# A third pair of buffers for rounded weights, conversion two jobs ahead from the last projection on, and the first spread sums landed in two parts

## Chip, cores, metric

The kernel runs on 1 core of one Trainium2 chip. The metric is the device time of one execution in microseconds (us); lower is better. All times below are us unless marked otherwise. Engines: PE does matmuls, ACT, DVE and POOL work on tensors in SBUF and PSUM, SP issues most of the DMAs.

## The reference

Two layers of a hybrid decoder on 16 learned meta tokens and 512 real ones (528 columns here, 1024 features). Cut to what matters for this change:

```python
proj = einsum('bld,dc->blc', rmsnorm(h, attn_norm_g), w_in)
fq, fk, fv, flog, rq, rk, rv, rg = split(proj)            # FoX group, retention group
logf = log_sigmoid(flog + b_fgate)
c = cumsum(logf, axis=1)                                  # the forget sums, one row per head
s = einsum('bhqd,bhkd->bhqk', q, k) * Dh**-0.5 + c[..., :, None] - c[..., None, :]
fox_out = softmax(mask(s)) @ v
ret_out = silu(rg) * groupnorm(retention(rotate(rq), rotate(rk), rv))
h = h + concatenate([fox_out, ret_out]) @ w_out
hn = rmsnorm(h, ffn_norm_g)
h = h + (silu(hn @ w_gate) * (hn @ w_up)) @ w_down
```

FoX has 8 heads of 64, retention 4 of 128; the feed-forward width is 2816. After both layers comes a last rmsnorm, and the meta tokens are dropped.

## The kernel before, in words

**Products in three parts.** Every float32 weight and activation is split into a rounded high part and the rest (`whi`, `wlo`; `xh`, `xl`), and each product is three matmuls, `xh*whi + xl*whi + xh*wlo` (lines 197 to 230, the matmul itself is L217). So each block of weights is first loaded raw, and then converted: `whi` is an ACT cast (L191), and `wlo` is a subtraction raw - `whi` (L194) on DVE in two pieces of 128x512, or on POOL in eight of 128x128 where the job has `pool`.

**Jobs.** Each 1024x128 block of `w_in`, `w_out`, `w_gate` and `w_up` that `dense_steps` handles is a job j with one raw buffer (ring of 3, loaded by SP with L158, 512 KB) and one pair `whi`, `wlo` (rings of 2, from the pool `wp`). While PE works on job j, its steps 1 and 4 convert the two halves of job j+1. So a raw buffer comes free when the job's conversion is done, and a pair when PE has used it. The later blocks of the feed-forward part come from another code path (lines 869 and 870, names `whi`, `wlo`, `fwhi`, `fwlo`).

**What orders the work.** PE's order is written out by hand: lists of steps are merged by position (`spread`, `merge`). The order on ACT, DVE, POOL and SP is made by a scheduler from what is ready when, with a few places of high priority; so another ring size or an earlier call moves instructions there. Each engine works in its own order and stops at the first instruction whose input is missing. For SP that means that a DMA behind a load waits until the load's raw buffer is free.

**The start of a layer.** `x` is normalised: ACT makes `xh` (L319) and squares, DVE makes `xl` (L320) and the running sum of squares `ss` (L340); `split` (L142 on ACT, L143 on DVE) makes `sqh` and `sql` of it, and PE sums over the partitions (L290). The forget weights are split into `pt` (L142), which POOL has cleared before (L364). In layer 1 POOL also clears the attention buffers (L85, L102) when it enters the attention phase. The first jobs of a layer are q, k and v of the first FoX pair; in layer 0 these are jobs 0, 1 and the ones that follow; in layer 1 q and k are converted by ACT and DVE, and v by ACT and POOL.

**The forget sums.** A scan (L399) makes the sums of all 8 heads, ACT writes them to DRAM (`cdr`, L401), and for each head SP spreads one row of them over 128 partitions (`bc`, L497, 264 KB). `scores` (from L492) needs `bc` in L514, which subtracts it from PE's scores (L507) and finds the row's minimum, `nmax`.

Of the kernel before, what the change touches and what calls it, by code (L numbers as in the profile page):

```python
# [11 lines left out]
F32R = mybir.dt.float32r  # L12
# [4 lines left out]
NK = D // 128  # L17
SEQ = 512
META = 16
# [20 lines left out]
def hybrid_kernel(ctx, tc, x_t, w_in, w_fl, w_out, w_gate, w_up, w_down, vecs, b_fg, rope, decay, mask, ident, out_t):  # L40
# [119 lines left out]

    def wring(tag):
        pool = phase["ffn"] if tag[0] == "f" else wp
        return pool.tile([128, NK, 128], F32R, name=tag, tag=tag, bufs=2)

    def convert(j, upto=NK, pinned=False):

        if j >= len(jobs):
            return
        job = jobs[j]
        fetch(j)  # L170
        if "make" in job:
            if "w" not in job:
                n = job["n"]
                hi, lo = (wring(job["ring"] + p) for p in ("whi", "wlo"))
                job["w"] = [(NK, hi, lo)]
                job["make"](hi[:, 0:n], lo[:, 0:n])
            return
        n = job["src"].shape[1]
        if "w" not in job:
            job["w"] = [(NK, *(job["own"]() if job["own"] else  # L180
                               [wp.tile([128, NK, 128], F32R, name=i, tag=i) for i in ("whi", "wlo")]))]
            job["split"] = 0
        sub = nc.gpsimd.tensor_sub if job["pool"] else nc.vector.tensor_sub
        while job["split"] < min(n, upto):
            c0 = job["split"]
            c1 = min(n, c0 + (2 if j < 2 and c0 < 4 else 4))
            size, hi, lo = job["w"][c0 // job["w"][0][0]]
            o = c0 % size
            hi, lo = hi[:, o:o + c1 - c0], lo[:, o:o + c1 - c0]
            with tc.high_priority() if j == 5 else ExitStack():  # L190
                pin(nc.scalar.copy(hi, job["raw"][:, c0:c1]), pinned)  # L191
            step = 1 if job["pool"] else c1 - c0
            for i in range(0, c1 - c0, step):
                pin(sub(lo[:, i:i + step], job["raw"][:, c0 + i:c0 + i + step], hi[:, i:i + step].bitcast(F32)), pinned)  # L194
            job["split"] = c1

    def dense_steps(src, parts, pool=False, banks=False, ahead=(1, 4), own=None, wait=None):

        j = len(jobs)
        jobs.append({"src": src, "pool": pool, "own": own})

        def chunk(k0, k, n, xs, cols, ps, done):
            def go():
                convert(j)
                if k == 0:
                    t = [psum_a() for _ in cols] if banks else psum()
                    ps.append(t)
                    ps.append(t if banks else [t[:, b] for b in range(2)])  # L210
                size = jobs[j]["w"][0][0]
                _, hi, lo = jobs[j]["w"][(k0 + k) // size]
                wk = (k0 + k) % size
                xh, xl = xs(k)
                for i, (w, x) in enumerate(((hi, xh), (hi, xl), (lo, xh))):
                    for b, (c0, c1) in enumerate(cols):
                        nc.tensor.matmul(ps[1][b][:, 0:c1 - c0], w[:, wk, :], x[:, c0:c1],  # L217
                                         start=(k == 0 and i == 0), stop=(k == n - 1 and i == 2))
                if k == n - 1:
                    done(ps[0]) if wait is None else wait.append(lambda: done(ps[0]))  # L220
                for half, at_step in enumerate(ahead):
                    if k0 + k == at_step:
                        convert(j + 1, 4 * half + 4)
            return go

        steps = []
        for k0, xs, n, cols, done in parts:
            ps = []
            steps += [chunk(k0, k, n, xs, cols, ps, done) for k in range(n)]
        return steps  # L230
# [239 lines left out]
    def fox_steps(g, st, ly, real):  # L470
# [21 lines left out]
        def scores(s, b):  # L492
            nq, nk, q0 = span(b)
            if b == blocks[0]:
                bc = at("bc", F32, bufs=2)
                hd = 2 * g + s
                nc.sync.dma_start(bc, ly["cdr"][hd:hd + 1, :].partition_broadcast(128))  # L497
                st["bc"] = bc
            bc = st["bc"]
            segs = FULL if nk == T else ((0, nk),)  # L500
            pt = take(pm_tiles, "pm") if b < 0 else p_tiles[b]
            mins = []
            normalise()
            for c0, c1 in segs:
                sc = psum_a()
                for i, kk in enumerate(st["k"][s]):
                    nc.tensor.matmul(sc[0:nq, 0:c1 - c0], st["q"][s][:, q0:q0 + nq], kk[:, c0:c1],  # L507
                                     start=(i == 0), stop=(i == 1))
                nm = tmp.tile([128, 1], F32, name="nmax", tag="nmax", bufs=6)
                with tc.high_priority():  # L510
                    if c1 == nk:
                        diag = sc[0:nq, c1 - c0 - nq:c1 - c0]
                        nc.vector.tensor_add(diag, diag, msk[0:nq, 0:nq])
                    nc.vector.tensor_tensor_reduce(pt[0:nq, c0:c1], sc[0:nq, 0:c1 - c0], bc[0:nq, c0:c1],  # L514
                                                   -1.0, 3.0e38, ALU.add, ALU.min, nm[0:nq])
                mins.append(nm)
            nmax = mins[0]
            if len(mins) > 1:
                nc.vector.tensor_tensor(nmax, mins[0], mins[1], ALU.min)
            if b < 0:  # L520
                rsum = tmp.tile([META, 1], F32, name="rsum", tag="rsum", bufs=4)
            else:
                if (s, b) == (0, 0):
                    st["sums"] = tmp.tile([128, NBLK, 2], F32, name="sums", tag="sums")
                rsum = st["sums"][:, b, s:s + 1]
            pr = pt[0:nq, 0:nk]
            nc.scalar.activation(pr, pr, AF.Exp, bias=nmax[0:nq], scale=-1.0, accum_out=rsum)  # L527
            info[s, b] = pt
            if b == NBLK - 1:
                st["ct"] = tmp.tile([32, NBLK, 32], F32, name="ct", tag="ct")  # L530
                nc.vector.transpose(st["ct"], p_tiles[NBLK][96:128, :, WP - 32:WP])
            if b < 0:
                info["open"] = (pr, rsum)
            elif (s, b) == todo[-1]:
                nc.vector.reciprocal(st["sums"], st["sums"])
                st["rows"] = tt("tq")
                nc.scalar.copy(st["rows"][:, 0:SEQ].rearrange("p (b s d) -> p b s d", b=NBLK, s=2),
                               st["sums"].unsqueeze(3).broadcast_to([128, NBLK, 2, 64]))
# [248 lines left out]
    def out_proj(l, rnd, mix, real):  # L787

        cols = REAL if real else FULL
        xs = lambda k: mix[k]["mix"]  # L790
        return sum([dense_steps(w_out[l, rnd, m2], [(4 * s, xs, 4, cols, add_h(2 * m2 + s, real)) for s in range(2)],
                                rnd == 0 or m2 < 2, rnd == 1 and m2 == 1) for m2 in range(NK // 2)], [])

    def ffn(l, st, real, last):
        QC = REAL if real else FULL
# [234 lines left out]
        for r, (f0, f1) in enumerate(ROUNDS):  # L1030
            for f in range(f0, f1):
                if f < PLAIN:
                    steps += dense_steps(w_gate[l, f], [(0, xs, NK, QC, g_done(f) if f else held.append)], banks=f == 1)
                    steps += dense_steps(w_up[l, f], [(0, xs, NK, QC, u_done(f))])
                    continue
                u = Unit(f)
                steps += u.head()
                for v in tails:
                    v.last()
                    steps += v.tail()  # L1040
                tails = []
                u.rest()
                steps += u.middle()
                if fills:
                    p, g0, g1 = fills.pop(0)
                    j = down_job(p, g0, g1)
                    steps += down(j, 0, 2 * p, g0, g1, not real)
                    u.last()
                    steps += u.tail()
                    steps += down(j, 1, 2 * p + 1, g0, g1, False)  # L1050
                else:
                    tails = [u]
            for p, g0, g1 in fills:
                j = down_job(p, g0, g1)
                for s in range(2):
                    steps += down(j, s, 2 * p + s, g0, g1, False)
            fills = [(p, f0, f1) for p in range(NK // 2)]
# [348 lines left out]
```

## Time and profile before

| What | Value |
|---|---|
| median of 3 runs | 1271.39 (1270.4 to 1271.77) |
| the profiled execution, its own time | 1271.32 |
| its span in the trace | 1269.5 |
| mean granted clock of PE | 0.999 |
| weight loads of `w_in`, issue to landing, median | 3.5 (54 loads of 512 KB) |
| spreading `bc`, issue to landing, median | 3.5 (16 of 264 KB) |

The span runs from the first to the last instruction of the trace; 1.8 of the execution's own time lie around it. "Busy" counts the time in which an engine has an instruction in work. In a timeline, a row gives the start, the time to the end of the group, the engine, the line, the operation with output and inputs, the count, and in brackets how long the engine had been idle ahead of it and what ended that. SPq is SP's queue: its long rows of several DMAs hold the waits between them.

### The profile page before, as it was taken

What the parts mean: (1) busy time and instruction counts of PE and PEld (TensorE: products, weight loads), DVE (VectorE), ACT (ScalarE), POOL (GpSimd) and SP (SyncE); (2) the same over time, 40 slices, a digit from 0 to 9 for tenths busy, and PEclk for the clock granted to TensorE, in tenths of its full rate; (3) what the DMA queues carried; (4) which work ended last, traced back from release to release, by engine and by line L of the source; (5) the groups of instructions that cost most, each with busy time, mean ns of one, the idle gap of its engine ahead of it and who ended that gap; (6) DMA issues with size and microseconds to landing.
All of it is one profiled execution on the core that took longest, in us unless ns stands there. A gap on an engine that the chain in (4) does not pass through costs nothing.

```text
span 1269.5 us, 23615 instructions
## 1 busy us (share of the span) xinstructions
PE 1255.6 (99%) x9271; PEld 1197.8 (94%) x9271; DVE 997.3 (79%) x1843; ACT 687.7 (54%) x1246; POOL 264.0 (21%) x522
## 2 busy tenths in 40 slices
PE   9999999999999999999999999999999999999997
PEld 8999999999999999999999989998789999999996
DVE  7877756779988888887786877567899888888866
ACT  6666545676444444444456665557764444444444
POOL 3355546420000000000025545454100000000000
PEclk9999999999999999999999999999999999999999
DMA  6222232223333333332323232222323333333321
GB/s 217 93 69 86 88 87 73 70 68 114 107 97 100 100 100 101 100 100 84 101 76 119 62 99 83 80 88 68 101 95 120 100 100 100 101 100 100 104 80 67
DMA packets 45680, 120.57 MB, mean 95 GB/s; under 512 B 5360, under 2 KB 12272, under 8 KB 45568
## 3 DMA queue, kind: packets, MB, share of 16 engines
q1 hardware_dynamic: 45104, 118.74, 29.8%
q8 instruction: 73, 1.20, 0.4%
q10 hardware_dynamic: 464, 0.32, 0.1%
q14 instruction: 39, 0.32, 0.1%
HBM read 116.91 MB, written 2.13 MB: 94 GB/s over the span
## 4 chain that ended last, share of the span: by engine, by line
PE 94%; DVE 3%; ACT 2%; DMA 1%; issue 0%; DVEq 0%; ACTq 0%
PE psd L217 30%; PE psa L881 18%; PE psd L1016 14%; PE psd L881 13%; PE psa L217 5%; PE psa L1016 4%; PE psa L418 2%; PE psa L573 2%; PE psa L507 2%; PE psa L730 1%; PE psa L700 1%; PE psa L379 1%; PE psa L290 0%; ACT whi L191 0%; DMA raw<-w_in 0%
## 5 line engine op out<-in xcount | busy, mean ns | idle before, releaser
L194 POOL TENSOR_TENSOR wlo<-raw,whi 128x128 fp32r<-128x128 f32 x504 | 258.8, 548 | 288.5 <-ACT whi L191 288.4
L217 PE MATMUL psd<-xh,whi 128*128 128x264 f32 (+1 forms) x792 | 196.2, 315 | 0.6 <-ACT whi L191 0.6
L217 PE MATMUL psd<-xh,wlo 128*128 128x264 f32 (+1 forms) x792 | 187.2, 304 | 0.0
L217 PE MATMUL psd<-xl,whi 128*128 128x264 f32 (+1 forms) x792 | 186.7, 303 | 0.4 <-DVE xl L320 0.4
L217 PEld LDWEIGHTS psd<-xh,whi 128*128 128x128 f32 x792 | 128.9, 190 | 5.7 <-ACT whi L191 1.3
L217 PEld LDWEIGHTS psd<-xh,wlo 128*128 128x128 f32 x792 | 127.5, 189 | 6.2 <-DVE wlo L194 0.4
L217 PEld LDWEIGHTS psd<-xl,whi 128*128 128x128 f32 x792 | 128.0, 189 | 4.8 <-DVE xl L320 0.8
L191 ACT CAST whi<-raw 128x512 fp32r<-128x512 f32 (+1 forms) x168 | 98.3, 613 | 49.5 <-PE psd L217 37.6
L869 ACT CAST whi<-raw 128x1024 fp32r<-128x1024 f32 (+2 forms) x62 | 54.9, 885 | 51.2 <-PE psd L881 39.9
L869 ACT CAST fwhi<-raw 128x1024 fp32r<-128x1024 f32 (+2 forms) x62 | 55.7, 898 | 47.5 <-PE psd L881 39.9
L1116 POOL TENSOR_TENSOR th<-th,e 128x544 f32<-128x544 f32 x1 | 1.4, 1366 | 359.2 <-DVE e L1136 359.2
L870 DVE TENSOR_TENSOR wlo<-raw,whi 128x1024 fp32r<-128x1024 f32 (+2 forms) x62 | 62.9, 1015 | 12.9 <-ACT whi L869 12.8
L85 POOL MEMSET kl<- 64x528 f32 x2 | 1.1, 534 | 345.4 <-PE psa L881 345.4
L870 DVE TENSOR_TENSOR fwlo<-raw,fwhi 128x1024 fp32r<-128x1024 f32 (+2 forms) x62 | 64.0, 1032 | 10.5 <-ACT fwhi L869 10.3
L881 PE MATMUL psa<-th,whi 128*128 128x264 f32 (+1 forms) x232 | 65.4, 282 | 0.0
L881 PE MATMUL psa<-th,wlo 128*128 128x264 f32 (+1 forms) x232 | 65.4, 282 | 0.0
L881 PE MATMUL psa<-tl,whi 128*128 128x264 f32 (+1 forms) x232 | 65.3, 282 | 0.0
L881 PE MATMUL psa<-th,fwhi 128*128 128x264 f32 (+1 forms) x224 | 63.4, 283 | 0.0
L881 PE MATMUL psa<-tl,fwhi 128*128 128x264 f32 (+1 forms) x224 | 63.3, 283 | 0.0
L881 PE MATMUL psa<-th,fwlo 128*128 128x264 f32 (+1 forms) x224 | 63.2, 282 | 0.0
L527 ACT ACTIVATE probs<-probs,nmax 128x144 f32<-128x144 f32 (+1 forms) x64 | 36.9, 576 | 44.2 <-DVE nmax L514 31.3
L947 ACT COPY e<-psa 128x264 f32<-128x264 f32 (+1 forms) x114 | 42.9, 376 | 28.3 <-PE psa L881 24.1
(340 smaller groups left out, 4030.2 us busy)
## 6 DMA issues: line engine op xcount, KB each, us to landing
raw<-w_in SPq DMA_DIRECT2D x54, 512.0 KB, 3.5
raw<-w_gate SPq DMA_DIRECT2D x44, 512.0 KB, 3.7
fraw<-w_up SPq DMA_DIRECT2D x38, 512.0 KB, 3.5
raw<-w_down SPq DMA_DIRECT2D x64, 256.0 KB, 2.8
raw<-w_out SPq DMA_DIRECT2D x16, 512.0 KB, 3.4
raw<-w_down SPq DMA_DIRECT2D x32, 192.0 KB, 2.4
bc<-cdr SPq DMA_DIRECT2D x16, 264.0 KB, 3.5
raw<-w_up SPq DMA_DIRECT2D x6, 512.0 KB, 3.5
```

Source lines behind the costliest of these rows:

```text
L191: pin(nc.scalar.copy(hi, job["raw"][:, c0:c1]), pinned)
L194: pin(sub(lo[:, i:i + step], job["raw"][:, c0 + i:c0 + i + step], hi[:, i:i + step].bitcast(F32)), pinned)
L217: nc.tensor.matmul(ps[1][b][:, 0:c1 - c0], w[:, wk, :], x[:, c0:c1], start=(k == 0 and i == 0), stop=(k == n - 1 and i == 2))
L418: nc.tensor.transpose(ps[:, 128 * j:128 * j + 128], src[:, o:o + 128], idt)
L507: nc.tensor.matmul(sc[0:nq, 0:c1 - c0], st["q"][s][:, q0:q0 + nq], kk[:, c0:c1], start=(i == 0), stop=(i == 1))
L527: nc.scalar.activation(pr, pr, AF.Exp, bias=nmax[0:nq], scale=-1.0, accum_out=rsum)
L573: nc.tensor.matmul(po[:, c0:SEQ], v[:, j, :], pp[:, j, META + c0:T], start=(j == 0 and i == 0), stop=(j == 4 and i == 1))
L869: nc.scalar.copy(hi, src)
L870: nc.vector.tensor_sub(lo, src, hi.bitcast(F32))
L881: nc.tensor.matmul(bank()[:, 0:b.shape[-1]], a[:, o + k, :], b, start=(fresh and k == 0 and i == 0), stop=(k == n - 1 and i == 2), skip_gr ...
L947: nc.scalar.copy(self.t["e"][:, i], self.t["x"][:, 0:w])
L1016: nc.tensor.matmul(v[:, 0:c1 - c0], a[:, s * n + k, :], b[:, c0:c1], start=(k == 0 and i == 0), stop=(k == n - 1 and i == 2))
```

## The change

Three edits. The ring of rounded weights gets three pairs instead of two, for all jobs but those of the feed-forward ring (whose tag begins with "f"). `dense_steps` has a new argument `far`: with it, steps 1 and 4 of job j also convert the halves of job j+2. It is set for the second round of the out projection and for the gate and up jobs of the first three feed-forward blocks. And for head 0 of each layer `bc` comes in two DMAs, of the columns 0 to 143 and 144 to 527.

```diff
     def wring(tag):
         pool = phase["ffn"] if tag[0] == "f" else wp
-        return pool.tile([128, NK, 128], F32R, name=tag, tag=tag, bufs=2)
+        return pool.tile([128, NK, 128], F32R, name=tag, tag=tag, bufs=2 if tag[0] == "f" else 3)
...
             job["w"] = [(NK, *(job["own"]() if job["own"] else
-                               [wp.tile([128, NK, 128], F32R, name=i, tag=i) for i in ("whi", "wlo")]))]
+                               [wring(i) for i in ("whi", "wlo")]))]
...
-    def dense_steps(src, parts, pool=False, banks=False, ahead=(1, 4), own=None, wait=None):
+    def dense_steps(src, parts, pool=False, banks=False, ahead=(1, 4), own=None, wait=None, far=False):
...
                     if k0 + k == at_step:
                         convert(j + 1, 4 * half + 4)
+                        if far:
+                            convert(j + 2, 4 * half + 4)
...
-                nc.sync.dma_start(bc, ly["cdr"][hd:hd + 1, :].partition_broadcast(128))
+                parts = ((0, META + 128), (META + 128, T)) if hd == 0 else ((0, T),)
+                for c0, c1 in parts:
+                    nc.sync.dma_start(bc[:, c0:c1], ly["cdr"][hd:hd + 1, c0:c1].partition_broadcast(128))
...
-                                rnd == 0 or m2 < 2, rnd == 1 and m2 == 1) for m2 in range(NK // 2)], [])
+                                rnd == 0 or m2 < 2, rnd == 1 and m2 == 1, far=rnd == 1) for m2 in range(NK // 2)], [])
...
-                    steps += dense_steps(w_gate[l, f], [(0, xs, NK, QC, g_done(f) if f else held.append)], banks=f == 1)
-                    steps += dense_steps(w_up[l, f], [(0, xs, NK, QC, u_done(f))])
+                    steps += dense_steps(w_gate[l, f], [(0, xs, NK, QC, g_done(f) if f else held.append)], banks=f == 1, far=True)
+                    steps += dense_steps(w_up[l, f], [(0, xs, NK, QC, u_done(f))], far=True)
```

PE's instructions stand in the same order in both kernels. On the other engines the conversions move. Three places follow, with the numbers that the program gives to its buffers; line numbers in the changed kernel are 2 higher from L295 on and 4 higher behind `scores`.

SP's queue in layer 0, before: loads of jobs (`raw_593` is j5, `raw_742` j6, `raw_862` j7, `raw_985` j8) and the spread sums `bc` (`bc_553` is head 0, `bc_751` head 1).

```order
L158 DMA raw_593<-w_in 128x1024
L158 DMA raw_742<-w_in 128x1024
L158 DMA raw_862<-w_in 128x1024
L497 DMA bc_553<-cdr0_424 128x528
L497 DMA bc_751<-cdr0_424 128x528
L158 DMA raw_985<-w_in 128x1024
```

The same place of SP's queue now, where `raw_594`, `raw_743`, `raw_863` and `raw_986` are j5 to j8:

```order
L158 DMA raw_594<-w_in 128x1024
L158 DMA raw_743<-w_in 128x1024
L158 DMA raw_863<-w_in 128x1024
L158 DMA raw_986<-w_in 128x1024
L501 DMA bc_553<-cdr0_424 128x144
L501 DMA bc_553<-cdr0_424 128x384
L501 DMA bc_752<-cdr0_424 128x528
```

The load of j8 has moved ahead of the sums of head 0. With three raw buffers, j7's load waits until j4 is converted, and j8's until j5 is.

POOL's queue at that time, before: the `wlo` of j3, j4 (`wlo_512`), j5 (`wlo_596`) and the two jobs behind.

```order
L194 TENSOR_TENSOR wlo_337<-raw_334,whi_336 128x128 x8
L194 TENSOR_TENSOR wlo_512<-raw_509,whi_511 128x128 x8
L194 TENSOR_TENSOR wlo_596<-raw_593,whi_595 128x128 x8
L194 TENSOR_TENSOR wlo_745<-raw_742,whi_744 128x128 x8
L194 TENSOR_TENSOR wlo_865<-raw_862,whi_864 128x128 x8
```

POOL's queue now, where j5 is `wlo_597`:

```order
L194 TENSOR_TENSOR wlo_337<-raw_334,whi_336 128x128 x8
L194 TENSOR_TENSOR wlo_512<-raw_509,whi_511 128x128 x4
L194 TENSOR_TENSOR wlo_597<-raw_594,whi_596 128x128 x8
L194 TENSOR_TENSOR wlo_512<-raw_509,whi_511 128x128 x4
L194 TENSOR_TENSOR wlo_746<-raw_743,whi_745 128x128 x8
```

The third pair is free from the start, so j5's eight operations stand between the two halves of j4. ACT's casts have moved in the same way.

POOL's queue at the start of layer 1, before: the clearing of the attention buffers (`kl`, `probs`, `vt`, `rs`, `pt`), then v (`wlo_8623`).

```order
L85 MEMSET kl0_8409 64x528
L85 MEMSET kl1_8410 64x528
L102 MEMSET probs_8413 128x4x16
L102 MEMSET vt0_8415 128x112
L102 MEMSET vt1_8416 128x112
L102 MEMSET rs00_8421 128x16
L102 MEMSET rs01_8422 128x16
L102 MEMSET rs10_8423 128x16
L102 MEMSET rs11_8424 128x16
L364 MEMSET pt0_8419 128x1024
L102 MEMSET pt1_8420 128x4x16
L194 TENSOR_TENSOR wlo_8623<-raw_8620,whi_8622 128x128 x8
```

And now, where v is `wlo_8624`:

```order
L194 TENSOR_TENSOR wlo_8624<-raw_8621,whi_8623 128x128 x8
L85 MEMSET kl0_8410 64x528
L85 MEMSET kl1_8411 64x528
L102 MEMSET probs_8414 128x4x16
L102 MEMSET vt0_8416 128x112
L102 MEMSET vt1_8417 128x112
L102 MEMSET rs00_8422 128x16
L102 MEMSET rs01_8423 128x16
L102 MEMSET rs10_8424 128x16
L102 MEMSET rs11_8425 128x16
L366 MEMSET pt0_8420 128x1024
L102 MEMSET pt1_8421 128x4x16
```

The conversion of v has moved from behind the clearing to ahead of it. ACT's cast into `pt` waits for the clearing, and ACT's cast `sqh` stands behind that cast, in both kernels.

## The prediction

> **What bounds the kernel now.** I read the page first (span, busy engines, the chain that ended last), then what PE waits for, then the timelines of SP, POOL, DVE, ACT and PE at the places where the order changes. The page:
>
> ```profile
> span 1269.5 us, 23615 instructions
> PE 1255.6 (99%) x9271; PEld 1197.8 (94%) x9271; DVE 997.3 (79%) x1843; ACT 687.7 (54%) x1246; POOL 264.0 (21%) x522
> PE 94%; DVE 3%; ACT 2%; DMA 1%; issue 0%; DVEq 0%; ACTq 0%
> L194 POOL TENSOR_TENSOR wlo<-raw,whi 128x128 fp32r<-128x128 f32 x504 | 258.8, 548 | 288.5 <-ACT whi L191 288.4
> ```
>
> PE is busy 99% of the span and 94% of the last chain. In the list of what PE waits for, this is the only row with a rounded weight of these jobs:
>
> ```profile
> PE psd L217 <- ACT whi L191: 0.6, 1, 0.6
> ```
>
> That one wait is the first matmul of the program, which this change doesn't touch; no row has PE waiting for `wlo`. So running conversion two jobs ahead, in the out projection and the gate and up loop, removes a wait that isn't there: its gain is 0. That holds for the third pair of buffers too. What is left to decide is whether the new order makes something late. PE's own order is the same in both kernels, so every change of the time is a wait that appears or goes.
>
> **Layer 0, the first spread sums (`bc`).** In before, SP issues weight loads j5, j6, j7 and then `bc`; job j7's buffer comes free when POOL has finished `wlo` of j4. In after, a fourth load (j8) stands ahead of `bc`, and POOL's work for j4 is cut in two with all eight operations of j5 in between. So SP reaches `bc` only after 16 POOL operations instead of 8.
>
> ```profile
> 20.47 10.64 SPq L158 DMA_DIRECT2D raw<-w_in  x3
> 36.83 0.81 SPq L497 DMA_DIRECT2D bc<-cdr  x2
> 25.29 5.47 POOL L194 TENSOR_TENSOR wlo<-raw,whi 128x128 fp32r<-128x128 f32 x8 [0.79 <-ACT whi L191]
> 37.51 3.46 POOL L194 TENSOR_TENSOR wlo<-raw,whi 128x128 fp32r<-128x128 f32 x8 [6.76 <-ACT whi L191]
> 36.83 3.20 DMA bc<-cdr
> 40.17 0.16 DVE L514 CUSTOM_DVE_ANT_0 pm<-psa,bc 16x16 f32<-16x16 f32 x1 [0.21 <-DMA bc<-cdr]
> 40.39 0.39 PE L507 MATMUL psa<-kh,qs 128*128 128x272 f32 x1 [0.46 <-DVE nmax L514]
> ```
>
> Here is the path. In before, j7's load goes out at 31.11 (end of the first row), 0.36 after POOL ends j4 at 30.76, and SP then has nothing to do but wait for the sums. `bc` goes out at 36.83, lands at 40.03, L514 starts at 40.17, and PE, which waits for it, goes on at 40.39. That is the kernel's true path (the chain has this DMA as a piece), and there is no slack: any delay of `bc` is a delay of PE.
>
> When does POOL finish j4 in after? At 30.76 it has done eight operations, four of j4 and four of j5; eight are left. Undisturbed they take 3.46 (second POOL row): 34.2. But DVE is not quiet then:
>
> ```profile
> 30.45 1.60 DVE L438 TENSOR_TENSOR qs<-tq,qs 64x528 fp32r<-64x528 f32 x2
> 33.11 0.68 DVE L398 TENSOR_TENSOR z<-z,z 8x528 f32<-8x528 f32 x1
> 34.07 1.24 DVE L399 TENSOR_TENSOR_SCAN z<-z 8x528 f32<-8x528 f32 x1
> 35.23 1.41 DVE L452 TENSOR_TENSOR kl<-tq,kh 64x528 fp32r<-64x528 f32 x2
> 664.18 2.50 POOL L194 TENSOR_TENSOR wlo<-raw,whi 128x128 fp32r<-128x128 f32 x2 [6.73 <-ACT whi L191]
> 664.36 1.40 DVE L399 TENSOR_TENSOR_SCAN z<-z 8x528 f32<-8x528 f32 x1
> 665.68 0.67 DVE L452 TENSOR_TENSOR kl<-tq,kh 64x528 fp32r<-64x528 f32 x1
> ```
>
> The last three rows are the same scan and the same `kl` in layer 1, with POOL beside them: two POOL operations, 0.87 by the undisturbed row, took 2.50, as the second, issued by about 664.6, stood through the scan and the first `kl`. DVE operations that read two SBUF tensors and POOL's subtractions do not run together. The first four rows hold 4.9 us of such work between 30.45 and 36.64. POOL gets one operation (0.43) in between two of them, and each that it gets pushes DVE back by some tenths (the scan took 1.40 beside POOL, 1.24 without). Letting them alternate, POOL does about five of its eight by 36.9 and the others by 38.1. The ends are 34.2 (nothing in the way) and 39.5 (it gets nothing until 36.6 and pays 0.3 more for DVE's next operations); the rate of the first POOL row, 0.68 for each, would give 36.2, but there DVE had less of this work in a stretch. I take 38.1.
>
> Then j7's load goes out at 38.15, j8's at 38.55, `bc` at 38.95 (0.4 for each issue, from the two of 0.81), and it lands behind two loads of 512 KB:
>
> ```profile
> fraw<-w_up SPq DMA_DIRECT2D x2, 512.0 KB, 4.7
> raw<-w_up SPq DMA_DIRECT2D x1, 512.0 KB, 3.4
> 911.40 0.33 SPq L158 DMA_DIRECT2D raw<-w_up  x1
> 911.78 0.90 SPq L905 DMA_DIRECT2D fraw<-w_up  x2
> 657.38 12.64 SPq L158 DMA_DIRECT2D raw<-w_in  x2
> 670.08 0.90 SPq L497 DMA_DIRECT2D bc<-cdr  x2
> DMA to landing us min/median/max: 4.1/4.1/4.1
> ```
>
> Three loads issued together: the first takes 3.4, the others a median of 4.7, so each load ahead adds about 1.25. In layer 1 (the last line is for the two `bc` in that place) one load right ahead of `bc` made its 3.2 into 4.1, that is +0.9. By the first, j7 lands at 41.55, j8 at 42.8, and the first part of `bc` (144 of 528 columns, 72 KB) at 43.0; by the second, 38.95 + 3.2 + 1.8 = 43.95 for a whole `bc`. I take 43.2, 3.17 later than 40.03. PE takes all of it: **+3.2**. Ends: with POOL done by 35.0, `bc` lands when it did (35.0 + 5.0), and the smaller first part gains at most the 0.2 that L514 idles, -0.2; with 39.5, +4.6. The weights themselves stay covered: in PE's order the second half of j4 is used only behind the matmul of 40.39, over 2 us after 38.1.
>
> The Trainium skill ("SBUF — State Buffer", Who interferes with whom) calls this an exclusive lock that goes to whoever issues first. The rows of 664 speak against its order: the POOL operation had been issued before `kl`, and `kl` still went first at 665.68. By the page POOL would have won there, 0.67 earlier, and the layer 0 term would be 2.5 instead of 3.2.
>
> **Layer 1, POOL's memsets.** In before POOL clears the attention buffers ahead of the conversion of v; in after the eight operations of v come first.
>
> ```profile
> 617.72 1.12 POOL L85 MEMSET kl<- 64x528 f32 x2 [345.37 <-PE psa L881]
> 619.33 0.95 POOL L364 MEMSET pt<- 128x1024 f32 x1
> 653.01 4.34 POOL L194 TENSOR_TENSOR wlo<-raw,whi 128x128 fp32r<-128x128 f32 x8 [32.64 <-ACT whi L191]
> 641.75 1.12 ACT L191 CAST whi<-raw 128x512 fp32r<-128x512 f32 x2
> 648.30 0.23 ACT L142 CAST pt<-wfr 128x64 fp32r<-128x64 f32 x1
> 649.71 0.63 ACT L142 CAST sqh<-ss 128x528 fp32r<-128x528 f32 x1 [1.19 <-DVE ss L340]
> 650.38 0.71 DVE L143 TENSOR_TENSOR sql<-ss,sqh 128x528 fp32r<-128x528 f32 x1 [0.56 <-ACT sqh L142]
> 651.14 0.51 PE L290 MATMUL psa<-sql,ones 128*128 128x264 f32 x2
> L320 DVE SCALAR_TENSOR_TENSOR xl<-h,vec,xh 128x528 fp32r<-128x528 f32 x4 | 3.1, 768 | 0.2 <-ACT xh L319 0.2
> L340 DVE TENSOR_TENSOR ss<-ss,sq 128x528 f32<-128x528 f32 x4 | 2.8, 706 | 0.0
> L194 DVE TENSOR_TENSOR wlo<-raw,whi 128x512 fp32r<-128x512 f32 x2 | 1.4, 690 | 0.0
> ```
>
> v's casts take the slot that k's have at 641.75, so POOL starts at about 642.3. The memsets and the clearing of `pt` come after v's eight: from 617.72 to the end of `pt` at 620.28 they need 2.56. Only then may ACT write `pt` (the cast at 648.30), and behind that cast stand `sqh`, DVE's `sql` and PE's L290, in that order. Slack: the `pt` cast may slip by 1.19, to 649.5, without moving `sqh`, so POOL must end v by 646.9.
>
> The last three rows are DVE's groups from 642 to 650. It loses the two subtractions of k (1.4 us), and keeps eight operations on two SBUF tensors (`xl` 3.1 and `ss` 2.8: 5.9 of the 8 us). Undisturbed, v ends at 645.8; by the row at 653.01 (4.34) at 646.6; alternating as above at 648.8; at 650 if DVE always goes first. I take 648.8, since DVE is fuller here than where those two rows were taken: `pt` clear at 651.35, cast to 651.6, `sqh` to 652.2, `sql` to 652.95, PE's `sql` matmuls at 653.0 instead of 651.14: **+1.9** (0 to +3.1; a gain of at most 0.1, by which the 0.51 is above the 0.40 of the other pairs).
>
> **The rest, at nothing.** One more DMA issue in each layer costs SP 0.4. In layer 1 the one load ahead of `bc` stays, and DVE idles 0.9 for `bc` there while no row shows PE waiting for it. The earlier conversions in the out projection and the gate and up loop move ACT and DVE work that PE doesn't wait for; I allow +-0.5 for small shifts there.
>
> **The sum.** 1271.32 (the profiled execution; the median of the runs is 1271.39) + 3.2 + 1.9 = 1276.4.
>
> **Rivals.**
> - Both covers hold: POOL runs nearly at its undisturbed rate, finishing j4 before 35.0 and v before 646.9. Then `bc` lands in smaller parts, -0.2, and layer 1 gives -0.1: 1271.32 - 0.3 = 1271.0, not slower. For: 504 POOL operations average 548 ns against 430. Against: the 2.50 at 664.18. Chance 0.13.
> - Only layer 0: v's conversion ends by 646.9, as the 4.34 of the row at 653.01 would have it. 1271.32 + 3.2 = 1274.5. Chance 0.25.
> - Only layer 1: 1273.2. It needs POOL done by 35.0 in layer 0 alone, where the blocking work is thickest. Chance 0.06.
> - The wait also costs clock. PE then stands for 3.6 us ahead of the matmul of 40.39. The start of the program shows its slow clock:
>
> ```profile
> 5.57 0.81 PE L217 MATMUL psd<-xh,whi 128*128 128x264 f32 x2 [0.62 <-ACT whi L191]
> 9.67 0.40 PE L217 MATMUL psd<-xh,whi 128*128 128x264 f32 x2
> 9.91 0.40 PE L217 MATMUL psd<-xl,whi 128*128 128x264 f32 x2
> ```
>
> Nine pairs took the 4.1 us from 5.57 to 9.67; at the 0.24 of the next one they take 2.2. One such stretch more is +1.9: 1278.3. Against: the wait of 0.46 that is there now is followed by a matmul of the usual 0.39, but it is far shorter. Chance 0.06.
>
> The Trainium skill ("TensorE: Matmul & The Clock Gate", Part 1) has the clock fall after an idle window of about 3.4 us, and the windows run freely; a gap of 3.6 could fill one whole window only by luck, so by it the time mostly stays 1276.4.
>
> Both waits, my forecast, get the remaining 0.5. The range goes from 1272.2 (each wait at about a sixth of its value) to 1279.0 (both upper ends, 4.6 + 3.1) and leaves out the first rival. About 0.2% (2.5 us) is what a measurement can tell: slower means above 1273.9, which is the forecast, most of "only layer 0" and the clock, less the part in which both waits are small.
>
> **What would show it.** Right: `bc` of head 0 issued near 38.9 and landing near 43, the POOL operations of j4 ending near 38, the L507 of 40.39 with 3 to 4 us of idle time ahead of it; in layer 1 POOL's memsets after the v conversion, ending near 651, and PE idle some 2 us ahead of L290. Wrong: `bc` issued by 37, or the `pt` cast at its old place; or a wait of PE somewhere else, in the out projection or the gate and up loop, that I have put at nothing.

## The result, and the profile after

| | median us | runs | ratio to before, 95% interval |
|---|---|---|---|
| before | 1270.89 | 6 (1270.3 to 1271.77) | |
| changed kernel | 1276.3 | 6 (1275.91 to 1277.33) | 1.0042 [1.0032, 1.0052] |

The changed kernel is slower by 5.4 us. Its profiled execution took 1277.33, the longest of the six; its span is 1275.5. The page and the list of what PE waits for show where to look:

```profile
span 1275.5 us, 23565 instructions
PE 1257.5 (99%) x9271; PEld 1200.1 (94%) x9271; DVE 992.5 (78%) x1843; ACT 685.1 (54%) x1246; POOL 267.5 (21%) x522
L194 POOL TENSOR_TENSOR wlo<-raw,whi 128x128 fp32r<-128x128 f32 x504 | 262.3, 555 | 622.7 <-ACT whi L191 622.6
```

```profile
PE psa L511 <- DVE nmax L518: 3.6, 1, 3.6
PE psa L292 <- ACT sqh L142: 0.8, 1, 0.8
PE psd L217 <- ACT whi L191: 0.5, 1, 0.5
PE psa L292 <- DVE sql L143: 0.2, 1, 0.2
```

The first row was 0.5 before; the second and fourth were not there. The third row is the first matmul of the program, as in before: no wait for a weight has gone, so nothing was won.

PE's order is the same in both kernels, so each of the 9271 matmuls can be set beside itself. The difference of the starts (after less before, by before's times) moves at few places: -0.9 by 9.67 (the slow matmuls at the program's start end earlier in this execution), +0.1 by 36, +3.2 in one step at the matmul of 40.39, +2.7 spread over the 6 us behind it, then -0.4. In the feed-forward part of layer 0 it drifts by +0.5 in all (one step of -0.2 and many small ones up). L290 at the start of layer 1 gives +0.9 and +0.35, and the feed-forward part of layer 1 gives 0.8 back. The last matmul is 5.75 late.

**Layer 0.** SP, POOL, DVE and PE, in this order:

```profile
21.03 17.35 SPq L158 DMA_DIRECT2D raw<-w_in  x4
38.43 1.39 SPq L501 DMA_DIRECT2D bc<-cdr  x3
```

```profile
21.67 19.66 POOL L194 TENSOR_TENSOR wlo<-raw,whi 128x128 fp32r<-128x128 f32 x32 [19.98 <-ACT whi L191]
```

```profile
33.26 1.23 DVE L401 TENSOR_TENSOR_SCAN z<-z 8x528 f32<-8x528 f32 x1
42.55 0.16 DVE L518 CUSTOM_DVE_ANT_0 pm<-psa,bc 16x16 f32<-16x16 f32 x1 [3.40 <-DMA bc<-cdr]
```

```profile
38.72 0.41 PE L217 MATMUL psd<-xh,wlo 128*128 128x264 f32 x2
42.77 0.60 PE L511 MATMUL psa<-kh,qs 128*128 128x272 f32 x1 [3.64 <-DVE nmax L518]
43.39 0.65 PE L217 MATMUL psd<-xh,whi 128*128 128x264 f32 x2
43.83 0.65 PE L217 MATMUL psd<-xl,whi 128*128 128x264 f32 x2
48.21 0.64 PE L217 MATMUL psd<-xl,whi 128*128 128x264 f32 x2
48.65 0.46 PE L217 MATMUL psd<-xh,wlo 128*128 128x264 f32 x2
49.54 0.41 PE L217 MATMUL psd<-xh,wlo 128*128 128x264 f32 x2
```

POOL now works without a break from 21.67. The 24th of its 32 operations, the last of j4, ends at 38.03, and SP's fourth load goes out at 38.05. `bc` follows at 38.43 instead of 36.83, and L518 starts at 42.55 instead of 40.17. PE stands for 3.64. When it goes on, its pairs of 128x264 take 0.65 instead of 0.41 and follow each other by 0.44 instead of 0.24, until 48.65: the slow clock of the program's start, a second time. The granted clock shows it. These are rows of three stretches of the changed kernel; each gives the stretch, its length, the busy time and count of PE, PEld, DVE, ACT and POOL, PE's granted clock, and the DMA's share and GB/s:

```profile
36.00:42.00 6.00, 3.13 (x27) 2.91 (x25) 2.60 (x7) 2.00 (x5) 5.33 (x12) 0.99 0.73 205
44.00:46.00 2.00, 2.00 (x11) 2.00 (x10) 0.93 (x5) 0.61 (x2) 0.00 (x0) 0.50 0.32 129
50.00:52.00 2.00, 2.00 (x19) 2.00 (x18) 1.77 (x8) 1.07 (x3) 0.19 (x1) 1.00 0.00 0
```

The records of the granted clock have it at 0.50 from 41.92 to 48.75, 6.83 in all. In before it stays at 1.00 there.

**Layer 1.** ACT, POOL and PE:

```profile
647.01 1.12 ACT L191 CAST whi<-raw 128x512 fp32r<-128x512 f32 x2
656.14 0.24 ACT L142 CAST pt<-wfr 128x64 fp32r<-128x64 f32 x1 [2.35 <-POOL pt L366]
656.29 0.63 ACT L142 CAST sqh<-ss 128x528 fp32r<-128x528 f32 x1
```

```profile
647.75 5.74 POOL L194 TENSOR_TENSOR wlo<-raw,whi 128x128 fp32r<-128x128 f32 x8 [385.68 <-ACT whi L191]
653.55 1.12 POOL L85 MEMSET kl<- 64x528 f32 x2
655.16 0.95 POOL L366 MEMSET pt<- 128x1024 f32 x1
```

```profile
656.97 0.51 PE L292 MATMUL psa<-sqh,ones 128*128 128x264 f32 x2 [0.77 <-ACT sqh L142]
657.71 0.51 PE L292 MATMUL psa<-sql,ones 128*128 128x264 f32 x2 [0.23 <-DVE sql L143]
```

v's eight operations take 5.74, the clearing follows, the cast into `pt` starts in the moment it ends, and `sqh` and `sql` are late by the rest.

### The profile page after: what moved, and what is told of

Read it like the earlier page. It is cut to its first block, busy times and chain, and to the rows that moved or that the text cites. A ratio compares the mean times of both kernels' runs of the same rounds, so it can differ in the third digit from the quotient of the medians.

```text
span 1275.5 us, 23565 instructions
## 1 busy us (share of the span) xinstructions
PE 1257.5 (99%) x9271; PEld 1200.1 (94%) x9271; DVE 992.5 (78%) x1843; ACT 685.1 (54%) x1246; POOL 267.5 (21%) x522
## 5 line engine op out<-in xcount | busy, mean ns | idle before, releaser
L194 POOL TENSOR_TENSOR wlo<-raw,whi 128x128 fp32r<-128x128 f32 x504 | 262.3, 555 | 622.7 <-ACT whi L191 622.6
L1027 DVE TENSOR_TENSOR h<-psd,h 128x512 f32<-128x512 f32 (+1 forms) x69 | 47.7, 691 | 12.9 <-PE psd L1020 12.7
```

The costliest lines, as they stand in the source:

```text
L1027: nc.vector.tensor_add(sv(h[m], real), pv(ps[0], real), sv(h[m], real))
```

## The experiments

The theory: the third pair, not the two-ahead conversion, costs at three places (the wait for `bc`, the slow clock behind it, the clearing in layer 1). The rivals: the two-ahead conversion or the two-part `bc` costs by itself, or the two-ahead conversion brings a gain that the waits hide. Times of one group of kernels come with runs of before on the same chip. The ratio is worked out from all runs of both, so it needn't be the quotient of the two medians.

| Kernel | median us (before beside it) | ratio, 95% interval |
|---|---|---|
| two-part `bc` only | 1270.98 (1270.45) | 1.0000 [0.9991, 1.0009] |
| third pair only | 1275.58 (1270.45) | 1.0038 [1.0025, 1.0051] |
| third pair from the last projection on | 1276.45 (1270.45) | 1.0044 [1.0031, 1.0056] |
| third pair for the two-ahead jobs only | 1280.08 (1270.45) | 1.0075 [1.0061, 1.0088] |
| changed kernel again | 1276.02 (1271.23) | 1.0040 [1.0026, 1.0053] |
| wait filled with matmuls | 1274.62 (1271.23) | 1.0032 [1.0019, 1.0044] |
| v on DVE | 1274.57 (1271.23) | 1.0028 [1.0017, 1.0039] |
| `bc` on ACT's queue | 1273.09 (1271.05) | 1.0016 [1.0008, 1.0025] |
| `bc` on ACT's queue, v on DVE | 1271.41 (1271.05) | 1.0003 [0.9994, 1.0012] |

**Two-part `bc` only.** Before, with the third edit alone:

```diff
-                nc.sync.dma_start(bc, ly["cdr"][hd:hd + 1, :].partition_broadcast(128))
+                parts = ((0, META + 128), (META + 128, T)) if hd == 0 else ((0, T),)
+                for c0, c1 in parts:
+                    nc.sync.dma_start(bc[:, c0:c1], ly["cdr"][hd:hd + 1, c0:c1].partition_broadcast(128))
```

> The kernel before with only the two-part landing of head 0's spread sums. Theory (the time goes to three places that the third pair makes: the wait for bc in layer 0, +3.3; slow clock after that wait, 0 to +2.7; POOL's clearing in layer 1, +1.3): no change, -0.2 to +0.3, since the load of j8 stays behind bc. Rival (the extra DMA itself delays SP's queue): +0.5 or more.

No change, as expected. PE's wait for `nmax` there was 0.7, against 0.5 in before, so the smaller first part gained nothing.

**Third pair only.** Before, with the first edit alone:

```diff
-        return pool.tile([128, NK, 128], F32R, name=tag, tag=tag, bufs=2)
+        return pool.tile([128, NK, 128], F32R, name=tag, tag=tag, bufs=2 if tag[0] == "f" else 3)
...
-                               [wp.tile([128, NK, 128], F32R, name=i, tag=i) for i in ("whi", "wlo")]))]
+                               [wring(i) for i in ("whi", "wlo")]))]
```

> The kernel before with only the third pair of buffers; conversion runs one job ahead everywhere and bc lands whole. Theory: all three places are made by the third pair, so the whole loss is here, +5.4 (4.3 to 6.7), with PE waiting about 4 us for bc in layer 0 as bc is whole. Rival (running conversion two jobs ahead is what costs): +2 or less.

The whole loss is here. In its PE timeline the wait is 2.64, not the 4 expected, and the slow pairs begin about a microsecond after it:

```profile
43.05 0.40 PE L507 MATMUL psa<-kh,qs 128*128 128x272 f32 x1 [2.64 <-DVE nmax L514]
43.89 0.41 PE L217 MATMUL psd<-xh,wlo 128*128 128x264 f32 x2
44.53 0.64 PE L217 MATMUL psd<-xl,whi 128*128 128x264 f32 x2
```

So the two-ahead conversion isn't needed for the loss. What it does by itself was still open.

**Third pair from the last projection on, and only for the two-ahead jobs.** The changed kernel with the third pair as a buffer of its own, for each third job; in the first of the two it is in use from the first two-ahead job to the end, in the second for the two-ahead jobs alone (the edit shown):

```diff
-    def wring(tag):
+    third = {"n": 0}
+
+    def wring(tag, far=False):
         pool = phase["ffn"] if tag[0] == "f" else wp
-        return pool.tile([128, NK, 128], F32R, name=tag, tag=tag, bufs=2 if tag[0] == "f" else 3)
+        if far:
+            third["n"] += tag == "whi"
+            if third["n"] % 3 == 0:
+                return pool.tile([128, NK, 128], F32R, name=tag, tag=tag + "3", bufs=1)
+        return pool.tile([128, NK, 128], F32R, name=tag, tag=tag, bufs=2)
...
-                               [wring(i) for i in ("whi", "wlo")]))]
+                               [wring(i, job["far"]) for i in ("whi", "wlo")]))]
...
```

> The changed kernel, but with the third pair in use only from the last projection of layer 0 on, and in layer 1 to the end. Theory: layer 0 is as before, no long wait and no slow clock behind it; only the clearing in layer 1 is left, +1.3 (0.7 to 1.8). Rival (the clock falls by itself or the cost is spread over the two-ahead conversions): +3 or more.

> The changed kernel, but with the third pair only for the jobs that convert two ahead (last projection, gate and up of the first three blocks). Theory: both starts of a layer are as before and running two ahead neither gains nor costs, 0 (-0.5 to +0.5). Rival 1 (two ahead gains something that the two waits hide): -1 or lower. Rival 2 (two ahead costs by itself): +1 or more.

Both expectations failed in the total. The parts on the known places held: neither kernel shows the long wait for `bc`, and L290 in layer 1 is late by 1.2 in the first, where the third pair is still in use there, and not in the second. But a new wait of 2.7 and 2.8 came up near 254. ACT's and PE's timelines of the second kernel there:

```profile
253.33 0.62 ACT L197 CAST whi<-raw 128x512 fp32r<-128x512 f32 x1 [5.18 <-DMA raw<-w_out]
253.86 0.47 ACT L142 CAST pt<-psa 128x384 fp32r<-128x384 f32 x1
```

```profile
256.39 3.07 PE L583 MATMUL psa<-pt,vv 128*128 128x512 f32 x10 [2.76 <-DVE pt L143]
260.67 0.64 PE L223 MATMUL psd<-xl,whi 128*128 128x264 f32 x2
```

The third buffer is empty when it is first used, so the scheduler put that job's cast ahead of attention's cast into `pt`. Its load had not come, ACT stood for 5.18, and PE waited for `pt`. It is the same mechanism at another place, an early conversion ahead of work that PE needs, with the slow clock behind it again. In layer 1 of the second kernel it came once more: ACT stood 2.96 for a load of `w_out`, and PE waited 0.9 and 1.6 near 880. So these two say nothing on the two-ahead conversion itself, and other runs had to.

**The changed kernel again.**

> The changed kernel unchanged, for a second profile and for the same chip as the two next runs. Theory: +5.4 (4.3 to 6.5); PE waits 3.6 for bc again, and the stretch of slow matmuls behind it may be shorter, longer or missing, as the single times of the kernel spread by 1.4. Rival (the slow matmuls belong to something fixed in the program): the same stretch of 5.9 us again.

PE's timeline:

```profile
42.46 0.40 PE L511 MATMUL psa<-kh,qs 128*128 128x272 f32 x1 [1.96 <-DVE nmax L518]
42.82 0.41 PE L217 MATMUL psd<-xh,whi 128*128 128x264 f32 x2
43.79 0.40 PE L217 MATMUL psd<-xl,whi 128*128 128x264 f32 x2
```

PE goes on at nearly the same time as in the first profile (42.77), but it came later, waited 1.96 instead of the 3.6 expected, and no slow pairs follow; the granted clock stays at 1.00. The span is 1272.5, 3.0 below that of the first profile. So the slow stretch isn't fixed in the program.

**The wait filled.** 24 matmuls with a zero weight ahead of the one that waits:

```diff
             normalise()
+            if not real and (g, s, b) == (0, 0, 1):
+                for i in range(24):
+                    nc.tensor.matmul(filler["ps"][i % 2][:, 0:HALF], filler["w"], ly["x"][0][0][:, 0:HALF],
+                                     start=False, stop=False)
             for c0, c1 in segs:
```

> The changed kernel with 24 matmuls of 128x264 by a zero weight, added to the sum that PE is working on, put where PE waits for bc in layer 0 (2.9 us of work; they add zero). Theory: the wait itself stays, as bc lands when it did, but PE isn't idle long, the matmuls behind it take 0.40 to 0.41, and the time is 0 to 2.7 below the changed kernel, +3.5 to +4.5 over before. Rival (the matmuls behind are slow for another reason, such as contention): slow matmuls and +5.4 as before.

PE's timeline:

```profile
40.45 3.09 PE L513 MATMUL psd<-xh,zw 128*128 128x264 f32 x24
43.38 0.29 PE L518 MATMUL psa<-kh,qs 128*128 128x272 f32 x1
43.63 0.41 PE L219 MATMUL psd<-xh,whi 128*128 128x264 f32 x2
```

The matmul behind it starts later than without the filling (43.38 against 42.46 and 42.77), and the time is still 1.4 below the changed kernel on the same chip (1276.02): work that does nothing pays, since no slow pairs follow. Over before it is 3.4, a little under the 3.5 to 4.5 expected. The two intervals overlap, so the 1.4 is a rough size. That the slow clock is gone is in the rows and in every run: PE's mean granted clock was 0.998 or 0.999 in all five runs with the filling, and 0.997 or less in eight of the eleven runs of the changed kernel without it.

**v on DVE.**

```diff
-        return [dense_steps(w_in[l, 3 * g + i], [(0, lambda k: ly["x"][k], NK, c, f)], g > 0 or (i == 2 and not first), i == 2,
+        return [dense_steps(w_in[l, 3 * g + i], [(0, lambda k: ly["x"][k], NK, c, f)], g > 0, i == 2,
```

> The changed kernel with the conversion of v of the first pair in layer 1 on DVE instead of POOL. Theory: POOL clears its buffers near 620 again, the cast into pt no longer waits, and L292 waits no more than 0.3 in all: 1.3 below the changed kernel. Rival (it is DVE's sums of squares that are late there): no gain or a loss, as DVE has 1.4 more to do.

POOL's timeline, then PE's in layer 0:

```profile
622.97 0.95 POOL L366 MEMSET pt<- 128x1024 f32 x1
656.70 4.33 POOL L194 TENSOR_TENSOR wlo<-raw,whi 128x128 fp32r<-128x128 f32 x8 [32.69 <-ACT whi L191]
```

```profile
42.17 0.40 PE L511 MATMUL psa<-kh,qs 128*128 128x272 f32 x1 [2.89 <-DVE nmax L518]
42.92 0.65 PE L217 MATMUL psd<-xl,whi 128*128 128x264 f32 x2
```

The clearing is early again, no wait of L292 is left in the list of PE's waits, and the time is 1.45 below the changed kernel. Layer 0 is as it was, slow pairs included.

**`bc` on ACT's queue**, alone and with v on DVE:

```diff
-                    nc.sync.dma_start(bc[:, c0:c1], ly["cdr"][hd:hd + 1, c0:c1].partition_broadcast(128))
+                    with ExitStack() if real or hd else tc.high_priority():
+                        (nc.sync if real or hd else nc.scalar).dma_start(bc[:, c0:c1], ly["cdr"][hd:hd + 1, c0:c1].partition_broadcast(128))
```

> The changed kernel, but the two parts of head 0's spread sums in layer 0 are issued by ACT behind the casts of j6, instead of by SP behind the loads of j7 and j8; nothing else moves. Theory: bc goes out near 37.2 instead of 38.4 and lands behind one load at most, near 40.7; PE's matmul behind the wait starts near 41.2 instead of 42.2 to 43.0, the wait is too short for slow clock, and the layer 1 term stays: +2.1 over before (1.5 to 2.8). Rival (the loss in layer 0 is POOL's and DVE's contention, not SP's order): no change from the changed kernel, +5.

> The run before with the conversion of v of layer 1 on DVE as well, so that the three places found are mended and the third pair and the two-ahead conversion stay everywhere. Theory: +0.8 (0.2 to 1.4), what is left of the wait for bc. Rival 1 (conversion two jobs ahead gains something that the waits hid): below before by 0.5 or more. Rival 2 (there is a fourth cost): +2 or more.

ACT's and PE's timelines of the first of the two:

```profile
36.09 0.84 ACTq L502 DMA_DIRECT2D bc<-cdr  x2
```

```profile
39.75 0.39 PE L512 MATMUL psa<-kh,qs 128*128 128x272 f32 x1 [0.57 <-DVE nmax L519]
40.35 0.41 PE L217 MATMUL psd<-xl,whi 128*128 128x264 f32 x2
```

`bc` goes out at 36.09, 1.1 earlier than expected, PE waits 0.57, close to the 0.46 of before, and the pairs stay at 0.41. POOL ends j4 as late as in the changed kernel, since SP's load of j8, which waits for it, goes out at 38.10. So POOL's lateness costs only by way of SP's queue, and the rival is out. What is left of the loss is 2.0. With v on DVE as well, the time is 1.0003 [0.9994, 1.0012] of before: third pair, two-ahead conversion and two-part `bc` are all in, and nothing is lost or won. That answers what the failed pair left open: the two-ahead conversion brings nothing that can be measured. It also leaves no room for a fourth cost above 0.12%, unless a gain of the same size stands against it; no run here separates such a pair. No version tried beats the kernel before.

## Why the prediction came out as it did

**The total.** 1276.4 was forecast, 1276.3 measured. But it is not the sum that was forecast: two terms were smaller, 2.1 to 2.4 and 1.3 instead of 3.2 and 1.9, and a third of 1.5 to 2.7, which was priced as an unlikely rival, came in most of the profiles and made up for them. That the total agrees to 0.1 is luck.

**No gain: right.** No wait for a weight went, because none was there; the last experiment shows it by the time.

**The wait for `bc`: right in kind, 3.2 forecast, 2.1 to 2.4 found.** The steps up to POOL held: j4 finished at 38.03 (38.1 forecast), since POOL and DVE alternate as the rows of layer 1 had shown. (The upper end of 39.5 doesn't follow from its own terms, 36.6 + 3.46 + 0.3 = 40.4, so the range should have reached 0.9 higher. And 31.11 in before is the end of the load's issue, which began at 30.78, 0.02 behind POOL.) The step that failed is "j7's load goes out at 38.15". The loads don't take the buffers in the order of the jobs, which is what the prediction and the section on the change went by: j7's went out at 35.44, 0.02 after POOL's 20th operation, the last of j5, and only j8's waited for j4. So `bc` stood behind one fresh load, not two, went out at 38.43 instead of 38.95, landed 4.0 later instead of 4.25, and PE went on at 42.77 and 42.46 in the two profiles of this kernel instead of 43.56. Set beside before, that matmul is 2.4 and 2.1 late.

**Layer 1: right in kind, 1.9 forecast, 1.3 found.** (1.2 to 1.35 in six profiles with this order, set beside before as above.) Here the mis-sized term is the 6.5 us given to v's conversion (642.3 to 648.8). It took 5.74. Everything behind it went as written: the clearing took 2.6, the cast into `pt` waited 2.35, and `sqh` and `sql` followed in ACT's and DVE's queues. Taking v off POOL removed it.

**The clock: wrong.** The rival got 0.06, because the only wait at hand was one of 0.46 without effect, and that says nothing on one of 3. In four profiles with the unfilled wait, slow pairs follow in three (waits of 2.64, 2.89 and 3.64, costing 1.6, 1.5 and 2.7) and not in the fourth (1.96). By the Trainium skill ("TensorE: Matmul & The Clock Gate", Part 1) the clock falls after an idle window of about 3.4 us, and the prediction took from it that 3.6 would do so only by luck. The runs differ: 2.64 was enough. Where the slow pairs came, the granted clock stood at 0.50 for 3.41 behind the two shorter waits and for 6.83 behind the longest. Without slow pairs the loss is about that of the filled kernel, 3.4 us; the medians of the changed kernel, where most runs have them, are at 4.8 and 5.4.

**The rule on the shared port.** The rows in layer 0 look as those of layer 1 did, against the order that the Trainium skill gives ("SBUF — State Buffer", Who interferes with whom): the POOL operation that was issued at 33.27, beside the scan of 33.26, took 2.14, through the scan and the first `kl` behind it, though `kl` was issued at 34.42. The prediction's alternative sum (2.5 for this term) comes nearer to what was found, but not for that reason, since POOL's end was as forecast.

**Left open.** What decides whether a given execution falls into the slow clock wasn't controlled. Its share can be read roughly from the mean granted clocks: all twelve runs of the third pair alone and of v on DVE are at 0.997 or less, eight of the eleven of the changed kernel, and two of the 47 runs of before that stand beside the experiments. Nor were the small steps followed that PE loses in the feed-forward part of layer 0 (0.5 to 0.6 in all nine profiles with a third pair) and gets back in that of layer 1 (0.5 to 0.8 in eight of them, nothing in the filled kernel). They come with the third pair alone as well, so they aren't shown to belong to the two-ahead conversion; they are about the +-0.5 that was allowed there, and nearly cancel.

## What to carry to other kernels

More buffers let a scheduler run work earlier, and earlier isn't free: an in-order queue stands at the first thing that isn't there, and what PE needs stands behind it. Before adding a buffer, look whether the profile has a wait for it at all, and then follow each engine's queue for what moves ahead of the shared small steps (a broadcast, a clearing). And a stall of PE of some 2.6 us or more (five of five here) should be priced with the slow matmuls behind it, not only with its own length.

## What the runs showed of the hardware

PE's granted clock fell to 0.50 at idle times of 2.64, 2.72, 2.76, 2.89 and 3.64 us, and not at 1.96, 1.63 or 0.57. It stayed there for 3.41 or 3.42 us in three of the five and for 6.82 or 6.83 in two. The length of the idle time alone doesn't set the moment: the clock fell 1.70 us after the idle time of 2.76 had begun, and 2.0 us after the one of 2.72 had ended. Filling the wait with matmuls of zeros kept the clock.

Some execution times of one kernel differ by the length of the slow stretch at the program's start: the granted clock came up at 9.63 in the profile of before and at 7.79 in the first of the changed kernel, which put the matmuls there 0.9 ahead. The wait for `bc`, whose end POOL and SP set, then took that gain back.
